# One 512-column product for both parts of a split activation, in a kernel of two transformer blocks

## The chip, the core and the metric

The kernel runs on one core of a Trainium2 chip. Five engines work side by side: TensorE multiplies (the profile lists its matmuls as PE and its weight loads as PEld), VectorE (DVE) and ScalarE (ACT) compute on SBUF and PSUM, GpSimd (POOL) computes on SBUF, and SyncE (SP) issues DMAs. The metric is the device time of one execution in microseconds, the median over runs; lower is better.

## What is computed

The input is one sequence of 256 tokens with 1024 features, in float32. The reference is two blocks in a row:

```
x = x + mixers(rms_norm(x)) @ w_out                      # block 1: block attention, gated linear attention
x = x + (silu(h_gate) * h_val) @ w_ffn_down              # h = causal_dwconv(rms_norm(x) @ w_ffn_up)
x = rms_norm(x)
x = x + (sum over 4 branches: gate * branch) @ w_out_2   # block 2: conv, spatial gating, two attentions
x = x + (silu(g) * u) @ w_ffn_out_2                      # g, u = split(rms_norm(x) @ w_ffn_in_2)
```

Both feed-forward layers have 2816 hidden features. Seen as tiles of 128 x 128, all the weights together are 1888 tiles, 118 pieces of 1 MB with 16 tiles each. An up projection has 44 x 8 = 352 tiles, a down projection 8 x 22 = 176, and an output projection 8 x 8 = 64.

## The kernel before

Activations stand with the features in the partitions and the 256 tokens (`T`) in the free dimension, 1024 features as `KD` = 8 chunks and 2816 as `KF` = 22. The products have to be more exact than one pass in the matmul type float32r, so each operand is kept as two float32r parts that add up to the float32: a rounded part (hi, h) and the rest (lo, l). A product of a weight tile with a chunk of activations is then three matmuls of 256 columns into the same PSUM columns, by `mm3`:

```
PE.matmul(ps, lh, rh, ...)   # weight hi, activation hi    L185
PE.matmul(ps, lh, rl, ...)   # weight hi, activation lo    L186
PE.matmul(ps, ll, rh, ...)   # weight lo, activation hi    L187
```

`fm` runs `mm3` over the chunks of one output tile. `fm_pair` runs two output tiles of a bank at once and leaves the last chunk of both to the end, because after a norm's sum that chunk is ready last. `tm` has tokens in the partitions of the result.

The weights are one stream, in the order in which they are used. SyncE's queue loads pieces of 1 MB into three buffers. `split_to` cuts a piece in two halves of 8 tiles; ScalarE casts a half to its hi part (L154), VectorE subtracts to get the lo part (L155). There are five buffers of hi and of lo, and a half is split `AHEAD` = 4 halves before its first tile is used. Engines take their instructions in an order that is fixed when the program is built: a scheduler runs through the program with estimated times and writes the order out for each engine.

PSUM has eight banks. Four are the rotating buffers `mm` of the main products, one bank each (`mm_tile`), four belong to the attention work (`at_tile`).

`Boundary` handles a norm between layers. `add(d, ps)` adds output tile d to the residual stream X (VectorE, L387), then `scaled` writes X times the norm's weights as hi (ScalarE, L282) and lo (VectorE, L283), without the norm's 1/rms; a sum of squares runs beside it. The next layer starts on these raw parts. In `gated_ffn` the first `HELD` = 6 hidden pairs j use the raw parts, and their results are multiplied by 1/rms (`rb`) afterwards, by VectorE straight from PSUM (tile `held`, L745). Meanwhile `normed` makes normed parts chunk by chunk: GpSimd multiplies by rb (L290), ScalarE and VectorE write hi and lo (L291, L292), and the hidden pairs from the seventh on use these. Each hidden pair j is 16 tiles into one bank, gate in the lower 256 columns and value in the upper. In block 2 `swiglu_emit` applies Silu to the lower half of the bank (L1102), multiplies by the upper (L1103), and `split_from` writes hi and lo of the hidden tile (L217, L218). The down projection runs 22 tiles for each of 8 output tiles; in block 2 its result is added to X (L1107) and sent out by DMA (L1108).

Hence the order of the second half of the program: branch products of block 2, second output projection, norm, second up projection, second down projection. Work of the attention parts runs between the tiles of the main stream in both mixers.

Of the kernel before, what the change touches and what calls it, by code (L numbers as in the profile page):

```python
# [26 lines left out]
HELD = 6  # L27
# [25 lines left out]
def block_kernel(ctx: ExitStack, tc: tile.TileContext, xT, wst, sm_d, cs_d, lv_d, gup_d, out, dbg=None):  # L53
# [73 lines left out]
    class Stream:  # L127
# [17 lines left out]
        def split_to(self, n):  # L145
            while self.split < min(n, 2 * N_PIECES):
                i, h = divmod(self.split, 2)
                self.load_to(i + 3)
                hi = parts.tile([128, 1024], F32R, name="hi", tag="hi")
                lo = parts.tile([128, 1024], F32R, name="lo", tag="lo")  # L150
# [8 lines left out]
                self.hl[self.split] = (hi, lo)  # L159
                self.split += 1  # L160

        def tiles(self, n=1):
            """The next n tiles of 128 x 128, side by side."""
# [5 lines left out]
            hi, lo = self.hl[h]  # L169
            return hi[:, t * 128:(t + n) * 128], lo[:, t * 128:(t + n) * 128]  # L170
# [13 lines left out]
    def mm3(ps, lh, ll, rh, rl, start, stop, **kw):  # L184
        PE.matmul(ps, lh, rh, start=start, stop=False, **kw)  # L185
        PE.matmul(ps, lh, rl, start=False, stop=False, **kw)  # L186
        PE.matmul(ps, ll, rh, start=False, stop=stop, **kw)  # L187

    def fm(ps, xh, xl, ks, start=True, stop=True, steps=0, **kw):
        ks = list(ks)  # L190
        for n, k in enumerate(ks):
            wh, wl = st.tiles()
            mm3(ps, wh, wl, xh[:, k, :], xl[:, k, :], start and n == 0, stop and n == len(ks) - 1, **kw)
            if n % 4 == 3:
                pump(steps)

    def fm_pair(ps, xh, xl, between=None):
        """Two tiles at once, the last chunk of both at the end."""
        for n, (a, k) in enumerate([(a, k) for a in range(2) for k in range(KD - 1)] + [(0, KD - 1), (1, KD - 1)]):
            wh, wl = st.tiles()  # L200
            mm3(ps[:, a * T:(a + 1) * T], wh, wl, xh[:, k, :], xl[:, k, :], n == 0, k == KD - 1,
                skip_group_check=True)
# [3 lines left out]
    def tm(dests, xh, xl, steps=0):  # L206
        """Columns of the next 16 tiles, with the tokens in the partitions."""
        ws = [st.tiles(2) for _ in range(KD)]
        for i, ps in enumerate(dests):
            t = slice(i * 128, (i + 1) * 128)  # L210
            for k, (wh, wl) in enumerate(ws):
                mm3(ps, xh[:, k, t], xl[:, k, t], wh, wl, k == 0, k == KD - 1)
                if k % 4 == 3:
                    pump(steps)

# [5 lines left out]
    def bcast(cols, n, width, wk, tag, bufs):  # L221
        """cols [128 tokens, n]: the rows [n * width, 128 tokens] that hold them."""
# [4 lines left out]
    def inv_sqrt(v, n, wk, root=False):  # L227
        """1 / sqrt(v) from the tables (a logarithm and an exponential, or a root), then a step of Newton's."""
# [20 lines left out]
    def token_sums(rows):  # L249
        """The sums of rows [128, T] over the partitions, with the tokens in the partitions: [128, 2]."""  # L250
# [29 lines left out]
    def scaled(k, g, xh, xl):  # L280
        """Chunk k of the residual stream times the norm's weights, without the norm's 1/rms."""
        a = S.activation(xh[:, k, :], X[:, k, :], AF.Identity, scale=g[:, k:k + 1])  # L282
        b = V.scalar_tensor_tensor(xl[:, k, :], X[:, k, :], g[:, k:k + 1], f32(xh[:, k, :]), op0=ALU.mult,  # L283
# [3 lines left out]
    def normed(rb, g, xh, xl, wk):  # L287
# [983 lines left out]
```

## Time and profile before

| | |
|---|---|
| runs | 761.25, 760.78, 760.6 us, median 760.78 us |
| profiled execution, first to last instruction | 758.6 us; this span is the only time shown of that execution |
| median less span | 2.2 us |
| TensorE matmul, weight load busy | 740.3 us, 723.2 us |
| VectorE, ScalarE, GpSimd busy | 544.2, 416.5, 113.6 us |
| granted TensorE clock, mean | 0.998 |

Busy shares of TensorE say little here: a matmul's record is longer than the distance to the next one, so records overlap. What one matmul costs is read from starts: the distance from one start to the next, or a stage's length divided by its tiles. A stage's length is read from the first start of its moving operand (mh for the second output projection, yh and xh for the second up projection, hh for the down projections).

### The profile page before, as it was taken

To read this page: it belongs to the slowest core of one execution; us is meant where nothing else is said; L and a number is where in the kernel's file an instruction comes from. 1 tells how busy PE (TensorE), PEld (TensorE's weight loads), DVE (VectorE), ACT (ScalarE), POOL (GpSimd) and SP (SyncE) were. 2 spreads that over 40 slices of the span, in tenths; PEclk is the share of its full clock that TensorE was granted. 3 is DMA by queue.
4 is the path that set the end of the run, shared out by engine and by line. 5 is a ranking of instruction groups with operands and counts; after the bars stand their busy time and mean duration, and the time that the engine had idled before them with its cause. 6 is when DMAs were issued, how large, how long until landed. Compare 5 with 4: busy or idle time off the path is not lost.

```text
span 758.6 us, 14593 instructions
## 1 busy us (share of the span) xinstructions
PE 740.3 (98%) x6042; PEld 723.2 (95%) x6042; DVE 544.2 (72%) x821; ACT 416.5 (55%) x673; POOL 113.6 (15%) x125
## 2 busy tenths in 40 slices
PE   8987899999999999999999999999999999999998
PEld 7987788999999999999998999999999999999998
DVE  6689955799998775556775777766988955555441
ACT  7453576568676665545547467445467644444330
POOL 3067200114312111212000001010223100000000
PEclk9999999999999999999999999999999999999999
DMA  8733231454545545544443444455445555545630
GB/s 303 291 112 111 74 133 72 167 183 152 219 171 199 190 168 193 197 168 167 162 172 111 139 145 163 170 182 204 167 164 209 184 183 198 175 172 201 204 125 22
DMA packets 19812, 127.51 MB, mean 168 GB/s; under 512 B 2321, under 2 KB 3746, under 8 KB 5026
## 3 DMA queue, kind: packets, MB, share of 16 engines
q1 hardware_dynamic: 19602, 126.56, 46.8%
q8 instruction: 47, 0.77, 0.4%
q14 instruction: 19, 0.16, 0.1%
q10 hardware_dynamic: 144, 0.02, 0.0%
HBM read 125.52 MB, written 1.05 MB: 167 GB/s over the span
## 4 chain that ended last, share of the span: by engine, by line
PE 90%; DVE 6%; issue 1%; DMA 1%; ACT 1%; SPq 0%
PE mm L186 28%; PE mm L185 28%; PE mm L187 28%; DVE lo L155 2%; DVE rob L648 1%; PE at L371 1%; DMA X<-in_x 1%; PE at L662 1%; DVE AT L505 1%; PE at L363 1%; DVE Qb L526 0%; DVE xl L283 0%; DVE AT L537 0%; PE at L892 0%; ACT hi L154 0%
## 5 line engine op out<-in xcount | busy, mean ns | idle before, releaser
L155 DVE TENSOR_TENSOR lo<-raw,hi 128x1024 fp32r<-128x1024 f32 (+1 forms) x236 | 296.3, 1259 | 138.2 <-ACT hi L154 137.4
L154 ACT CAST hi<-raw 128x1024 fp32r<-128x1024 f32 (+1 forms) x236 | 244.0, 1039 | 225.6 <-PE mm L186 179.4
L185 PE MATMUL mm<-yh,hi 128*128 128x256 f32 x800 | 226.4, 284 | 0.1
L186 PE MATMUL mm<-yl,hi 128*128 128x256 f32 x800 | 226.1, 283 | 0.0
L187 PE MATMUL mm<-yh,lo 128*128 128x256 f32 x800 | 226.0, 283 | 0.0
L185 PE MATMUL mm<-xh,hi 128*128 128x256 f32 x544 | 154.4, 285 | 1.4 <-ACT hi L154 1.4
L186 PE MATMUL mm<-xl,hi 128*128 128x256 f32 x544 | 155.0, 286 | 0.1
L187 PE MATMUL mm<-xh,lo 128*128 128x256 f32 x544 | 154.1, 285 | 1.0 <-DVE lo L155 1.0
L186 PEld LDWEIGHTS mm<-yl,hi 128*128 128x128 f32 x800 | 153.1, 192 | 0.7 <-issue 0.6
L185 PEld LDWEIGHTS mm<-yh,hi 128*128 128x128 f32 x800 | 152.8, 192 | 0.9 <-issue 0.7
L187 PEld LDWEIGHTS mm<-yh,lo 128*128 128x128 f32 x800 | 153.1, 192 | 0.1
L185 PEld LDWEIGHTS mm<-xh,hi 128*128 128x128 f32 x544 | 104.4, 192 | 2.2 <-ACT hi L154 1.8
L187 PEld LDWEIGHTS mm<-xh,lo 128*128 128x128 f32 x544 | 104.0, 192 | 2.2 <-DVE lo L155 1.6
L186 PEld LDWEIGHTS mm<-xl,hi 128*128 128x128 f32 x544 | 104.3, 192 | 1.3 <-DVE xl L283 0.5
L186 PE MATMUL mm<-hl,hi 128*128 128x256 f32 x352 | 98.4, 280 | 0.0
L187 PE MATMUL mm<-hh,lo 128*128 128x256 f32 x352 | 98.4, 280 | 0.0
L185 PE MATMUL mm<-hh,hi 128*128 128x256 f32 x352 | 98.1, 280 | 0.0
L186 PEld LDWEIGHTS mm<-hl,hi 128*128 128x128 f32 x352 | 66.2, 188 | 0.0
L187 PEld LDWEIGHTS mm<-hh,lo 128*128 128x128 f32 x352 | 66.2, 188 | 0.0
L185 PEld LDWEIGHTS mm<-hh,hi 128*128 128x128 f32 x352 | 66.0, 188 | 0.0
L277 POOL TENSOR_TENSOR ssa<-ssa,sq 128x256 f32<-128x256 f32 x20 | 18.8, 942 | 119.9 <-ACT sq L276 119.3
L771 POOL TENSOR_TENSOR cv<-cv 128x256 f32<-128x256 f32 x22 | 22.5, 1025 | 82.8 <-DVE cv L768 73.2
(333 smaller groups left out, 960.5 us busy)
## 6 DMA issues: line engine op xcount, KB each, us to landing
raw<-in_w SPq DMA_DIRECT2D x115, 1024.0 KB, 4.8
raw<-in_w SPq DMA_DIRECT2D x3, 512.0 KB, 8.2
out<-X SPq DMA_DIRECT2D x8, 128.0 KB, 1.9
sm<-in_sm SPq DMA_DIRECT2D x1, 814.5 KB, 11.9
X<-in_x SPq DMA_DIRECT2D x3, 256.0 KB, 7.1
cs<-in_cs SPq DMA_DIRECT2D x1, 706.0 KB, 11.2
raw<-in_w SPq DMA_DIRECT2D x2, 256.0 KB, 4.0
X<-in_x SPq DMA_DIRECT2D x2, 128.0 KB, 3.3
```

What stands on the lines that cost most here:

```text
L154: a = S.copy(hi[:, c:c + step], raw[:, c:c + step])
L155: b = V.tensor_tensor(lo[:, c:c + step], raw[:, c:c + step], f32(hi[:, c:c + step]), op=ALU.subtract)
L185: PE.matmul(ps, lh, rh, start=start, stop=False, **kw)
L186: PE.matmul(ps, lh, rl, start=False, stop=False, **kw)
L187: PE.matmul(ps, ll, rh, start=False, stop=stop, **kw)
L277: (V if self.n >= 6 else G).tensor_tensor(self.s, self.s, q, op=ALU.add)
L363: PE.transpose(pts[hd][:, j * 128:(j + 1) * 128], Ps[hd][:, j * 128:(j + 1) * 128], ident)
L371: PE.matmul(o, vs_[hd][0], PTs[hd][:, 0:256], start=True, stop=False, skip_group_check=True)
L505: V.tensor_scalar(AT[:, n // 4, n % 4, :], ident, dg[:, n:n + 1], None, op0=ALU.mult)
L648: V.tensor_tensor(b[o:o + 64, :], p[i:i + 64, :], sinr[i:i + 64, :], op=ALU.mult)
L662: PE.matmul(ps[:, c:c + n], qb[:, a, hd, i * 128:(i + 1) * 128], kT[:, a, :n], start=True, stop=False, skip_group_check=True)
L771: G.tensor_tensor(c[0], c[0], c[1], op=ALU.mult)
```

## The change

In four places, the down projections of both blocks, the second up projection and the second output projection, the two products that share the weight's hi part become one. For that the two parts of an activation now stand side by side, `[128, k, 2, T]` (class `Pair`, names `xx`, `yy`, `hh`, `mm_`), and the first matmul takes both as 512 columns; its result fills a whole bank, hi times hi in the lower 256 columns and hi times lo in the upper. The third product, lo weights with the hi activations, adds to the upper half. The two halves of a bank are summed afterwards: at a residual sum by two additions of VectorE instead of one, and in the second up projection by a ScalarE copy of the upper halves of two banks and one VectorE addition of the lower ones. There the 1/rms of the first six hidden pairs moves to GpSimd. All other places keep three matmuls of 256 columns.

PSUM's four `mm` buffers become two buffers of two banks (`mm_pair`). `mm_tile` gives out the two banks of such a buffer one after the other, so a buffer comes free when both banks have been read. The hi and lo parts of a weight half become one tile `hl` with five buffers, and in block 2's mixers two tiles (`u8a`, `u8b`) become one (`u16`). Elsewhere the diff renames (`xh, xl` to `x`, `mm3` to `mm_parts`) and drops comments.

```
-    mmp = ctx.enter_context(tc.tile_pool(name="mmp", bufs=4, space=PSUM))
+    mmp = ctx.enter_context(tc.tile_pool(name="mmp", bufs=2, space=PSUM))
+    spare = []
+    def mm_pair():
+        del spare[:]
+        return mmp.tile([128, 2, 512], F32, name="mm", tag="mm")
     def mm_tile():
-        return mmp.tile([128, 512], F32, name="mm", tag="mm")
+        if not spare:
+            p = mm_pair()
+            spare.append(p[:, 1, :])
+            return p[:, 0, :]
+        return spare.pop()
...
+    def both(ps, x, k, last):
+        w, b = st.tiles(), x.both(k)
+        PE.matmul(ps, w[:, 0, :], b.rearrange("p a t -> p (a t)"), start=(k == 0), stop=False, skip_group_check=True)
+        PE.matmul(ps[:, T:], w[:, 1, :], b[:, 0, :], start=False, stop=last, skip_group_check=True)
+    def fb(ps, x, n):
+        for k in range(n):
+            both(ps, x, k, k == n - 1)
+    def fb_pair(pss, x, between=None):
+        for n, (a, k) in enumerate([(a, k) for a in range(2) for k in range(KD - 1)] + [(0, KD - 1), (1, KD - 1)]):
+            both(pss[:, a, :], x, k, k == KD - 1)
+            if between and n == KD:
+                between()
+    def add_halves(dst, ps):
+        for a in range(2):
+            V.tensor_tensor(dst, dst, ps[:, a * T:(a + 1) * T], op=ALU.add)
...
         def add(self, d, ps):
-            V.tensor_tensor(X[:, d, :], X[:, d, :], ps, op=ALU.add)
-            behind = scaled(d, self.g, self.h, self.l)
+            if ps.shape[1] > T:
+                add_halves(X[:, d, :], ps)
+            else:
+                V.tensor_tensor(X[:, d, :], X[:, d, :], ps, op=ALU.add)
+            behind = scaled(d, self.g, self.raw)
...
-    def gated_ffn(nb, emit, finish):
+    def gated_ffn(nb, emit, finish, banks=False):
...
+                if banks:
+                    ps = mm_pair()
+                    if j == 0:
+                        fb_pair(ps, x, nb.sums)
+                    else:
+                        for a in range(2):
+                            fb(ps[:, a, :], x, KD)
...
+                if banks:
+                    t = wk.tile([128, 2, T], F32, name="held", tag="held", bufs=3)
+                    S.copy(t, ps[:, :, T:])
+                    V.tensor_tensor(t, t, ps[:, :, :T], op=ALU.add)
+                    if j < HELD:
+                        G.tensor_tensor(t, t, nb.rb[:, None, :].to_broadcast([128, 2, T]), op=ALU.mult)
+                    ps = t.rearrange("p a t -> p (a t)")
...
             for d in range(KD):
                 ps = mm_tile()
-                fm(ps[:, :T], hh, hl, range(KF))
-                finish(d, ps[:, :T], wk)
+                fb(ps, h, KF)
+                finish(d, ps, wk)
...
-        ps = mm_tile()
-        fm_pair(ps, mh, ml)
+        ps = mm_pair()
+        fb_pair(ps, m)
         for d in range(KD):
-            if d > 1:
-                ps = mm_tile()
-                fm(ps[:, :T], mh, ml, range(KD))
-            nb_.add(d, ps[:, T:] if d == 1 else ps[:, :T])
+            nb_.add(d, ps[:, d, :] if d < 2 else last)
+            if 0 < d < KD - 1:
+                last = mm_tile()
+                fb(last, m, KD)
...
     def second_end(d, ps, wk):
-        V.tensor_tensor(X[:, d, :], X[:, d, :], ps, op=ALU.add)
+        add_halves(X[:, d, :], ps)
         nc.sync.dma_start(out=out[:, d, :], in_=X[:, d, :])
...
-    gated_ffn(nb_, swiglu_emit, second_end)
+    gated_ffn(nb_, swiglu_emit, second_end, True)
```

## Rows read from the trace of the kernel before

**Rows 1.** Page, part 1: busy time of each engine, share of the span, instructions.
```profile
PE 740.3 (98%) x6042; PEld 723.2 (95%) x6042; DVE 544.2 (72%) x821; ACT 416.5 (55%) x673; POOL 113.6 (15%) x125
```

**Rows 2.** What TensorE waited for: total us, times, longest us.
```profile
PE at L533 <- DVE Qb L526: 10.0, 3, 4.6
PE mm L185 <- ACT hi L154: 1.4, 2, 1.2
```

**Rows 3.** Stretches: us, busy PE, PEld, DVE, ACT, POOL, clock, DMA share, GB/s.
```profile
544.20:566.00 21.80, 21.80 (x195) 21.80 (x194) 18.10 (x31) 12.20 (x22) 4.74 (x5) 1.00 0.42 147
566.00:693.10 127.10, 127.10 (x1060) 127.05 (x1059) 83.82 (x113) 67.28 (x102) 9.52 (x9) 1.00 0.53 191
```

**Rows 4.** Matmuls of one line by moving tile: ns min/median/max, first and last start.
```profile
L185 PE MATMUL mm<-mh,hi x64: 276/276/286, 544.2 to 565.6; 128*128 128x256 f32 x64
L185 PE MATMUL mm<-yh,hi x96: 280/283/468, 566.0 to 600.6; 128*128 128x256 f32 x96
L185 PE MATMUL mm<-hh,hi x176: 277/280/282, 693.1 to 754.7; 128*128 128x256 f32 x176
```

**Rows 5.** Timeline of TensorE: start us, us; the four 512-column products of line 932.
```profile
423.51 0.39 PE L932 MATMUL at<-h,nlater 128*128 128x512 f32 x1
423.74 0.28 PE L185 MATMUL mm<-yh,hi 128*128 128x256 f32 x1
423.86 0.28 PE L186 MATMUL mm<-yl,hi 128*128 128x256 f32 x1
...
428.53 0.39 PE L932 MATMUL at<-l,nlater 128*128 128x512 f32 x1
428.87 0.28 PE L185 MATMUL mm<-yh,hi 128*128 128x256 f32 x1
...
452.89 0.39 PE L932 MATMUL at<-h,nlater 128*128 128x512 f32 x1
453.23 0.28 PE L187 MATMUL mm<-yh,lo 128*128 128x256 f32 x1
...
460.18 0.39 PE L932 MATMUL at<-l,nlater 128*128 128x512 f32 x1
460.51 0.28 PE L187 MATMUL mm<-yh,lo 128*128 128x256 f32 x1
```

**Rows 6.** Timeline of TensorE: products with four-column weights (21 more between).
```profile
353.56 0.28 PE L186 MATMUL at<-yl,wfh 128*4 128x256 f32 x1
...
356.12 0.28 PE L187 MATMUL at<-yh,wfl 128*4 128x256 f32 x1
```

**Rows 7.** Groups by form: busy us, mean ns, then idle before and its releaser.
```profile
L1049 DVE TENSOR_TENSOR gate<-mm,rb 128x512 f32<-128x512 f32 x16 | 11.0, 689 | 6.1 <-PE mm L187 6.1
L387 DVE TENSOR_TENSOR X<-X,mm 128x256 f32<-128x256 f32 x24 | 9.5, 414 | 13.6 <-PE mm L187 13.6
L154 ACT CAST hi<-raw 128x1024 fp32r<-128x1024 f32 x232 | 241.7, 1046 | 224.8 <-PE mm L186 179.4 <-issue 31.6 <-PE mm L187 8.9
L519 ACT ACTIVATE E<-Dl 128x512 f32<-128x512 f32 x6 | 3.8, 632 | 11.3 <-DVE Dl L517 6.8 <-DVE Qb L526 4.5
L521 POOL TENSOR_TENSOR Kl<-gqk,E 128x512 f32<-128x512 f32 x6 | 9.1, 1516 | 0.2 <-ACT E L519 0.2
```

**Rows 8.** Timeline of VectorE, the end of the program.
```profile
755.26 0.42 DVE L1107 TENSOR_TENSOR X<-X,mm 128x256 f32<-128x256 f32 x1 [7.32 <-PE mm L187]
```

**Rows 9.** Timeline of VectorE around the second output projection's end.
```profile
553.22 1.23 DVE L155 TENSOR_TENSOR lo<-raw,hi 128x1024 fp32r<-128x1024 f32 x1 [2.66 <-ACT hi L154]
554.97 1.08 DVE L387 TENSOR_TENSOR X<-X,mm 128x256 f32<-128x256 f32 x3 [0.52 <-PE mm L187]
...
569.28 0.48 DVE L283 SCALAR_TENSOR_TENSOR yl<-X,sm,yh 128x256 fp32r<-128x256 f32 x1 [0.58 <-ACT yh L282]
```

**Rows 10.** Timeline of GpSimd behind that projection.
```profile
580.34 5.00 POOL L290 TENSOR_TENSOR xt<-X,rb 128x256 f32<-128x256 f32 x4 [14.17 <-DVE rb L242]
...
590.78 0.86 POOL L290 TENSOR_TENSOR xt<-X,rb 128x256 f32<-128x256 f32 x1 [0.76 <-DVE xl L292]
```

More of the change, by code (lines that the diff above doesn't have):

```diff
@@ L182, in block_kernel, with __init__, both @@
     V.tensor_copy(causalb, cst("causal"))
[L184 to L189, printed above, removed]
+    class Pair:
+        def __init__(self, t):
+            self.t, self.h, self.l = t, t[:, :, 0, :], t[:, :, 1, :]
+        def both(self, k):
+            return self.t[:, k]
@@ new lines, in fb, with fm @@
+    def fb(ps, x, n):
[9 more added lines that the diff above has]
+            V.tensor_tensor(dst, dst, ps[:, a * T:(a + 1) * T], op=ALU.add)
+    def fm(ps, x, ks, start=True, stop=True, steps=0, **kw):
@@ L190, in fm, with fm_pair @@
         ks = list(ks)
         for n, k in enumerate(ks):
-            wh, wl = st.tiles()
-            mm3(ps, wh, wl, xh[:, k, :], xl[:, k, :], start and n == 0, stop and n == len(ks) - 1, **kw)
+            mm_parts(ps, st.tiles(), x.both(k), start and n == 0, stop and n == len(ks) - 1, **kw)
             if n % 4 == 3:
                 pump(steps)
-    def fm_pair(ps, xh, xl, between=None):
+    def fm_pair(ps, x, between=None):
         for n, (a, k) in enumerate([(a, k) for a in range(2) for k in range(KD - 1)] + [(0, KD - 1), (1, KD - 1)]):
-            wh, wl = st.tiles()
-            mm3(ps[:, a * T:(a + 1) * T], wh, wl, xh[:, k, :], xl[:, k, :], n == 0, k == KD - 1,
-                skip_group_check=True)
+            mm_parts(ps[:, a * T:(a + 1) * T], st.tiles(), x.both(k), n == 0, k == KD - 1, skip_group_check=True)
@@ L381, in __init__ @@
             self.g, self.then = g, then or new_x
-            self.h, self.l = (first or new_y)()
+            self.raw = (first or new_y)()
             self.ss = SumSq(nwk, "a")
@@ L443, in block_kernel @@
             for d in range(4):
-                wh, wl = st.tiles()
-                mm3(pss[d // 2][:, d % 2 * T:(d % 2 + 1) * T], wh, wl, xh[:, k, :], xl[:, k, :],
-                    k == 0 and d % 2 == 0, k == KD - 1, skip_group_check=True)
+                mm_parts(pss[d // 2][:, d % 2 * T:(d % 2 + 1) * T], st.tiles(), x.both(k),
+                         k == 0 and d % 2 == 0, k == KD - 1, skip_group_check=True)
         r = rstd_cols(token_sums(ss.s), 2, 1.0 / D, nwk)
@@ L687, in block_kernel @@
                 ps = mm_tile()
-                fm(ps[:, :T], xh, xl, range(KD), steps=2)
+                fm(ps[:, :T], x, range(KD), steps=2)
                 rotary(ps, a, is_q)
@@ L695, in block_kernel @@
             ps = mm_tile()
-            fm(ps[:, :T], xh, xl, range(KD), steps=2)
+            fm(ps[:, :T], x, range(KD), steps=2)
             V.tensor_tensor(sg[:, e, :], ps[:, :T], rb, op=ALU.mult)
@@ L711, in block_kernel @@
                 a = accs[d // 2]
-                fm(a[:, (d % 2) * T:(d % 2 + 1) * T], yh, yl, range(4 * half, 4 * half + 4),
+                fm(a[:, (d % 2) * T:(d % 2 + 1) * T], y, range(4 * half, 4 * half + 4),
                    start=(half == 0 and d % 2 == 0), stop=(half == 1), steps=2, skip_group_check=True)
@@ L847, in proj @@
             for j in range(2):
-                fm(ps[:, j * T:(j + 1) * T], xh, xl, range(KD), steps=steps)
+                fm(ps[:, j * T:(j + 1) * T], x, range(KD), steps=steps)
             return ps.rearrange("p (c t) -> p c t", c=2)
-        q4 = wk.tile([128, 2, 2, 2, T], F32, name="q4", tag="u8a")
+        qkv = wk.tile([128, 14, T], F32, name="qkv", tag="u16")
+        q4 = qkv[:, 0:8, :].rearrange("p (n a h) t -> p n a h t", n=2, a=2)
         G.memset(q4, 0.0)
         qf, qs = q4[:, 0], q4[:, 1]
-        kv4 = wk.tile([128, 3, 2, T], F32, name="kv4", tag="u8b")
-        ks, vfx, vs = (kv4[:, n] for n in range(3))
+        ks, vfx, vs = (qkv[:, 8 + 2 * n:10 + 2 * n, :] for n in range(3))
         kf = wk.tile([128, 2, 2, T], F32, name="kf")
```

125 lines of the change are left out of this document (61 added, 64 removed).

## The prediction

> **What bounds the kernel now.** I start with the busy times [rows 1]: TensorE's matmuls and weight loads both cover nearly the whole span. Records overlap, so this shows only that TensorE is always at work, not at what speed. Next, what TensorE waited for [rows 2]: 10 us on VectorE inside the linear attention of the first block, 1.4 us on weight casts, and no entry at all for a PSUM buffer that was not free. Then the stretches of the changed stages [rows 3]: in the second output projection and the second up projection TensorE and its loads are busy from edge to edge at a granted clock of 1.00, VectorE 18.1 of 21.8 us and 83.8 of 127.1 us. So these stages last as long as their matmuls follow each other, and the price of a tile is a stage's length over its tiles. From first starts [rows 4]: the up projection runs from 566.0 (yh) to 693.1 (hh), 127.1 us / 352 = 0.361 us a tile; the down projection's first products start from 693.1 to 754.7, 175 steps, 0.352 us; the output projection takes 566.0 - 544.2 = 21.8 us / 64 = 0.341 us. A third of 0.361 is 0.120 us for one 256-column product.
>
> **What the change does to a tile.** It removes one matmul and one weight load of three and keeps the columns: 512 + 256 instead of 3 x 256. It pays only if something in those 0.120 us belongs to the matmul and not to its columns. The trace has four 512-column float32r products, each between products of 256 [rows 5]. The first starts at 423.51 and the next at 423.74: 0.23 us, less than 2 x 0.12. So 256 more columns cost 0.11, and about 0.01 is paid once per matmul. The change's pattern is exactly such a pair, one product of 512 and the 256 behind it. From the start of the 512 to the start of what follows the 256 the four pairs take 0.35, 0.34, 0.34 and 0.33 us. I take 0.343: single distances are read to 0.01, and a steady pattern of pairs may not do better than isolated ones. Bounds: 0.350 and 0.330, the longest and the shortest.
>
> The Trainium skill ("TensorE: Matmul & The Clock Gate", Back-to-back issue gap) speaks against the change: a matmul costs N / 2.4 + 2.5 ns, so one matmul less saves 2.5 ns a tile, an estimated 1.9 us over 768 tiles. The trace disagrees with its size, 0.120 us where it gives 0.109 for 256 columns.
>
> Is the extra the weight load, then? Products with four-column weights [rows 6] go from 353.56 to 356.12 in 22 steps, 0.116 us each: almost the same with hardly any load. So the load is not what a 256-column product waits for, and hiding more of it brings little.
>
> Sum for TensorE, each tile at 0.343: up projection 352 x 0.018 = 6.3 us; both down projections 352 x 0.009 = 3.2 us (the first has the same 176 tiles, and I take the second's pace for both); output projection 64 x -0.002 = -0.1 us. Together 9.4 us. At 0.350: 3.9 + 0.7 - 0.6 = 4.0 us; at 0.330: 10.9 + 7.7 + 0.7 = 19.3 us.
>
> **What it adds.** Every residual sum gets a second addition. One of 128 x 256 from PSUM takes 414 ns [rows 7].
>
> At the end of the program nothing covers it: the last addition starts right behind the last matmul [rows 8], then comes the last DMA. +0.4 us.
>
> In the first down projection a chunk has 22 tiles, 7.5 us, and the norm behind it still has fourteen tiles before it needs the last chunk: hidden.
>
> In the second output projection two things can wait. First, PSUM: there are now two buffers of two banks, and d = 4 needs the buffer of d = 0 and 1 back. It starts after 32 tiles, at 544.2 + 32 x 0.341 = 555.1. VectorE's first residual additions start at 554.97, because VectorE stands before a weight subtraction (553.22) for 2.66 us [rows 9]. With four additions of 0.41 us, TensorE would wait up to 1.5 us if this order stays, nothing if the scheduler puts them first. I take 0.7. Second, the last chunk for the next layer: its lo part is written by 569.76 [rows 9] and needed after fourteen tiles, at 566.0 + 14 x 0.361 = 571.1, 1.3 us of slack; at the faster pace 1.0 us. Eight more additions are 3.3 us on an engine with 3.7 us free. Bounds: no wait when only its own 0.4 us is added, 2.3 us when all 3.3 arrive there. I take 0.7. Behind those additions stand weight subtractions, but four halves of weights (32 tiles, 11 us) are ready ahead.
>
> In the second up projection a hidden pair takes 16 x 0.343 = 5.5 us. VectorE has 83.8 / 22 = 3.8 us of work in it and gets one addition of 512 columns, 0.69 us (L1049 in [rows 7]); that is 4.5, and less where it gives up the 1/rms product. ScalarE has 67.3 / 22 = 3.1 us and gets a copy of 512 columns, by the nearest row 0.63 us (L519 in [rows 7]): 3.7. Both are hidden under the matmuls with 1 us to spare; without that cover each 0.1 us beyond 5.5 would cost 2.2 us over 22 pairs. The copy and the addition free the PSUM buffer within some 3 us, and TensorE needs it 5.5 us later.
>
> The 1/rms products on GpSimd (1.5 us each for 512 columns, L521 in [rows 7]) share it with the eight products of the norm, which run from 580.34 to 591.6 [rows 10]. Taken in between they cost nothing; a bad order is a rival below. I take 0.3 us.
>
> In the mixers a mm buffer now returns when both its banks are read. No wait of TensorE for such a buffer shows before [rows 2]; VectorE waits for TensorE to fill them (6.1 us at L1049 in [rows 7]). Bounds 0 and about 1 us; I take nothing. The cast of a new weight half waits for the lo product too now, 0.12 us later; ScalarE already waits 179 us for TensorE there (L154 in [rows 7]), under cover of the four halves. Loads come a twentieth faster, on DMA engines that are half idle [rows 3]. A scheduler that writes a new order in the first block can move a microsecond either way; it has no term.
>
> Costs: 0.4 + 0.7 + 0.7 + 0.3 = 2.1 us. Net 9.4 - 2.1 = 7.3 us.
>
> The span of the profiled execution is 758.6 us and the median of the runs 760.8; the 2.2 us lie outside the first and last instruction and stay. Forecast: 760.8 - 7.3 = 753.5 us.
>
> **The rivals.** *Columns alone set the pace.* Then a 512-column product is 2 x 0.12 = 0.24 us, a tile stays at 0.36 or 0.35, and only the costs are left: 760.8 + 2.1 = 762.9 us, slower. It decides from 0.24 on. For it: the fixed part is one hundredth of a microsecond, read from four places, and none of the four has its moving operand in the x or y tiles that the up projection reads. Against it: none of the four pairs reaches 0.36. By the 2.5 ns a matmul of the Trainium skill (the section named above) it would be an estimated 761.0 us; no row here shows a distance that small over the columns' time.
>
> *The fixed part vanishes.* If with two loads under 768 columns only columns count, a tile takes 3 x 0.11 = 0.33 us: -19.3 + 2.1, 743.6 us. For it: one pair of four reads 0.33, and a lo load has all of a 512-column product to hide under. Against it: four-column loads still gave 0.116, and in the first pair 0.12 followed the 0.23.
>
> *GpSimd comes late in the second up projection.* If it does all eight norm products first, the first 1/rms product ends at 591.6 + 1.5 = 593.1, Silu and product (0.4 us each, as L387 in [rows 7]) at 593.9. Tile `held` has three buffers, so the copy of the fourth pair starts there and its PSUM buffer is free at 593.9 + 0.63 + 0.69 = 595.2; the sixth pair would start at 566.0 + 5 x 5.5 = 593.5. TensorE waits 1.7 us, and as much again if casts queue behind the waiting Silu on ScalarE and the weights run out. In place of the 0.3 us that is 3.4 us: 756.6 us. For it: four norm products already run back to back as soon as rb is there [rows 10]. Against it: they also wait for their readers, and gaps open between them.
>
> **How the numbers follow.** Forecast 0.70, with a range of its own from 748 (a tile of 0.335) to 759 (0.350 and these costs); columns alone 0.08; the fixed part vanishes 0.12; GpSimd late 0.10. Leaving out 0.08 above and most of the 0.12 below, the range is 745 to 759.5 us. A measurement of this kernel can tell about 0.2%, 1.5 us: faster is below 759.3, slower above 762.3. The forecast (0.68 of 0.70), the vanishing part (0.12) and most of GpSimd's case (0.08) are faster, together 0.88. Same: 0.03 of the columns, 0.02 of GpSimd, 0.01 of the forecast, 0.06. Slower: 0.05 of the columns, 0.01 of the forecast, 0.06.
>
> **What would show it.** Right: in the second up and the down projections a 512-column product is followed after 0.22 to 0.23 us and a 256 after 0.11 to 0.12; the up stage lasts near 121 us and each down projection near 60.4; the last matmul is followed by two additions. Wrong: 0.24 behind a 512; a wait of TensorE for a reader of mm or for a lo part near the second output projection of more than 3 us; GpSimd as releaser in front of Silu; or a first block whose length moves by more than 2 us. The prediction fails if the four pairs are no measure for operands in other tiles.

## The result and the profile after

The changed kernel takes 819.4 us (median of 4 runs, 817.98 to 820.5) where the kernel before takes 760.7 us on the same chip: ratio 1.0772, 95% interval [1.0757, 1.0788]. It is slower by 58.7 us. The forecast was 753.5 us, and no rival went past 763.

The page of the changed kernel first: busy times of TensorE and VectorE, and the granted clock of TensorE in 40 slices of the span.

```profile
PE 754.8 (92%) x5274; PEld 696.9 (85%) x5274; DVE 567.4 (69%) x861; ACT 429.4 (52%) x695; POOL 117.5 (14%) x131
...
PEclk9999999979999889999999999999999999999999
```

TensorE has 768 matmuls fewer than in [rows 1], as the change says, and its busy share fell from 98% to 92%. The clock row falls below 9 in three slices (164 to 184 and 266 to 307 us); its mean is 0.976 against 0.998. What TensorE waited for (engine, tile and line, releaser: us in total, times, longest us):

```profile
PE mm L205 <- DVE cv L820: 13.2, 3, 4.5
PE mm L205 <- DVE held L798: 9.7, 2, 6.1
PE mm L205 <- ACT hl L165: 8.5, 5, 2.2
...
PE mm L213 <- DVE X L229: 3.2, 3, 1.5
PE mm L213 <- DVE held L792: 2.7, 2, 2.2
```

L205 is the first of the three 256-column products of `mm_parts`; L213 and L214 are the 512 and the 256 of the new `both`. L820 (convolution), L798 and L792 (`held`, in the first and in the second block) and L229 (residual sum) are VectorE's reads of an `mm` buffer; L165 casts weights. So TensorE now waits for PSUM, in stretches that the change does not even convert: L205 is the unchanged form. In [rows 2] there is no such entry.

Now the stages by windows (us, then busy time of PE, PEld, DVE, ACT and POOL, clock, DMA share, GB/s). The kernel before: first up, first down, mixers of block 2, second down; its other two stages are in [rows 3].

```profile
150.10:278.50 128.40, 128.20 (x1060) 127.32 (x1059) 117.08 (x179) 88.54 (x147) 31.76 (x32) 1.00 0.52 185
278.50:340.30 61.80, 61.80 (x529) 61.80 (x528) 36.87 (x44) 31.84 (x47) 10.68 (x12) 1.00 0.53 188
340.30:544.20 203.90, 203.90 (x1649) 196.49 (x1649) 149.09 (x229) 111.14 (x163) 19.77 (x24) 1.00 0.46 161
693.10:754.90 61.80, 61.80 (x529) 61.80 (x528) 25.32 (x27) 19.48 (x20) 0.00 (x0) 1.00 0.39 135
```

The changed kernel: first up, first down, mixers of block 2, second output projection, second up, second down.

```profile
150.40:316.60 166.20, 134.02 (x1013) 131.99 (x1011) 110.95 (x170) 86.84 (x141) 25.94 (x31) 0.91 0.38 134
316.60:391.30 74.70, 71.35 (x416) 62.73 (x417) 42.35 (x56) 33.94 (x51) 11.12 (x13) 0.98 0.47 168
391.30:598.80 207.50, 203.82 (x1633) 194.51 (x1632) 149.49 (x234) 111.06 (x163) 17.80 (x24) 1.00 0.45 158
598.80:624.20 25.40, 23.16 (x130) 19.54 (x129) 21.54 (x36) 13.38 (x23) 4.21 (x5) 1.00 0.48 166
624.20:752.30 128.10, 125.19 (x709) 108.31 (x708) 99.58 (x126) 77.50 (x121) 19.19 (x15) 1.00 0.51 181
752.30:814.40 62.10, 61.13 (x353) 53.54 (x351) 28.57 (x35) 19.90 (x21) 0.00 (x0) 1.00 0.39 134
```

The first up projection went from 128.4 to 166.2 us and the first down projection, whose first tiles run among the last of the up, from 61.8 to 74.7: +50.7 of the span's +60 us. Mixers and output projection add 3.6 us each, the second up 1.0, the second down 0.3, the end 0.5 and the part ahead of the first up projection 0.3. Two windows there have a clock under 1.00. Its levels are 2.4 and 1.2 GHz, so 0.91 over 166.2 us is some 30 us at the lower one, and 0.98 over 74.7 us some 3.

What such a wait looks like, on TensorE's timeline (start us, us, instruction, in brackets the idle time and its releaser):

```profile
264.06 0.28 PE L207 MATMUL mm<-yy,hl 128*128 128x256 f32 x1
268.87 0.55 PE L205 MATMUL mm<-yy,hl 128*128 128x256 f32 x1 [4.53 <-DVE cv L820]
269.22 0.41 PE L206 MATMUL mm<-yy,hl 128*128 128x256 f32 x1
269.43 0.41 PE L207 MATMUL mm<-yy,hl 128*128 128x256 f32 x1
```

4.5 us of nothing, then products 0.21 us apart where they were 0.12: the clock had fallen to 1.2 GHz. ScalarE around it (L818 reads a half of a hidden pair's bank for the convolution, L165 casts weights):

```profile
252.87 0.56 ACT L818 ACTIVATE cv<-mm,sm 128x256 f32<-128x256 f32 x1 [0.41 <-DVE cv L820]
...
263.66 0.56 ACT L818 ACTIVATE cv<-mm,sm 128x256 f32<-128x256 f32 x1 [1.83 <-PE mm L207]
264.12 1.98 ACT L165 CAST hl<-raw 128x1024 fp32r<-128x1024 f32 x2
266.00 0.56 ACT L818 ACTIVATE cv<-mm,sm 128x256 f32<-128x256 f32 x1
```

And VectorE (L819 and L820 read the bank, L166 subtracts weights):

```profile
264.25 0.48 DVE L819 SCALAR_TENSOR_TENSOR cv<-mm,sm,cv 128x255 f32<-128x255 f32 x1 [1.17 <-ACT cv L818]
264.77 0.48 DVE L820 SCALAR_TENSOR_TENSOR cv<-mm,sm,cv 128x254 f32<-128x254 f32 x1
265.19 2.36 DVE L166 TENSOR_TENSOR hl<-raw,hl 128x1024 fp32r<-128x1024 f32 x2
267.46 0.87 DVE L819 SCALAR_TENSOR_TENSOR cv<-mm,sm,cv 128x255 f32<-128x255 f32 x2
268.25 0.86 DVE L820 SCALAR_TENSOR_TENSOR cv<-mm,sm,cv 128x254 f32<-128x254 f32 x2
```

Between 253.4 and 263.7 ScalarE reads no bank (the rows left out are casts and SBUF work). A pair takes 5.8 us in the kernel before (128.4 us / 22). Here the reads of two pairs come in one burst, the next burst starts 10 us after its end, and inside it two casts (264.12) and two subtractions (265.19) stand ahead of the read that TensorE needs. Distances of more than 1 us between starts come twelve times in the first up and down projections and sum to 38.7 us. The first is the longest, 6.34 us; the next four are 4.81, 4.81, 4.39 and 3.90 us. The first two end with L798. From 211 us on they come about every second hidden pair: four end with L820 (2.7 to 4.8 us), the other six with a weight cast, L165 (1.1 to 2.5 us).

### The profile page after: what moved, and what is told of

Read it like the earlier page. It is cut to its first block, busy times and chain, and to the rows that moved or that the text cites. A ratio compares the mean times of both kernels' runs of the same rounds, so it can differ in the third digit from the quotient of the medians.

```text
span 818.6 us, 13059 instructions
## 1 busy us (share of the span) xinstructions
PE 754.8 (92%) x5274; PEld 696.9 (85%) x5274; DVE 567.4 (69%) x861; ACT 429.4 (52%) x695; POOL 117.5 (14%) x131
## 4 chain that ended last, share of the span: by engine, by line
PE 76%; DVE 14%; ACT 4%; issue 3%; DMA 1%; POOL 1%; SPq 0%; ACTq 0%; POOLq 0%; DVEq 0%
PE mm L213 20%; PE mm L205 14%; PE mm L207 13%; PE mm L206 13%; PE mm L214 10%; DVE hl L166 4%; ACT hl L165 2%; ACT cv L818 1%; DVE cv L819 1%; DVE rob L690 1%; DVE xx L334 1%; DVE cv L820 1%; DMA X<-in_x 1%; PE at L413 1%; DVE X L229 1%
## 5 line engine op out<-in xcount | busy, mean ns | idle before, releaser
L166 DVE TENSOR_TENSOR hl<-raw,hl 128x1024 fp32r<-128x1024 f32 (+1 forms) x236 | 292.2, 1244 | 131.6 <-ACT hl L165 131.0
L165 ACT CAST hl<-raw 128x1024 fp32r<-128x1024 f32 (+1 forms) x236 | 243.5, 1040 | 187.7 <-PE mm L207 106.5
L205 PE MATMUL mm<-yy,hl 128*128 128x256 f32 x704 | 202.4, 289 | 21.9 <-DVE cv L820 13.2
L206 PE MATMUL mm<-yy,hl 128*128 128x256 f32 x704 | 202.3, 288 | 0.0
L207 PE MATMUL mm<-yy,hl 128*128 128x256 f32 x704 | 201.2, 287 | 0.0
L205 PEld LDWEIGHTS mm<-yy,hl 128*128 128x128 f32 x704 | 137.4, 196 | 24.5 <-issue 15.5
L206 PEld LDWEIGHTS mm<-yy,hl 128*128 128x128 f32 x704 | 137.8, 196 | 0.5 <-issue 0.2
L207 PEld LDWEIGHTS mm<-yy,hl 128*128 128x128 f32 x704 | 137.5, 196 | 0.5 <-issue 0.4
L213 PE MATMUL mm<-hh,hl 128*128 128x512 f32 x352 | 124.3, 397 | 6.0 <-ACT hl L165 2.5
L205 PE MATMUL mm<-xx,hl 128*128 128x256 f32 x288 | 86.1, 299 | 15.8 <-DVE held L798 9.7
L214 PE MATMUL mm<-hh,hl 128*128 128x256 f32 x352 | 98.9, 282 | 0.0
L213 PE MATMUL mm<-xx,hl 128*128 128x512 f32 x256 | 90.8, 399 | 0.7 <-DVE held L792 0.5
L207 PE MATMUL mm<-xx,hl 128*128 128x256 f32 x288 | 84.3, 294 | 1.4 <-DVE hl L166 1.4
L213 PEld LDWEIGHTS mm<-hh,hl 128*128 128x128 f32 x352 | 66.7, 190 | 21.9 <-ACT hl L165 3.0
L206 PE MATMUL mm<-xx,hl 128*128 128x256 f32 x288 | 84.0, 292 | 0.0
L205 PEld LDWEIGHTS mm<-xx,hl 128*128 128x128 f32 x288 | 57.5, 200 | 18.2 <-DVE held L798 6.3
L214 PE MATMUL mm<-xx,hl 128*128 128x256 f32 x256 | 71.9, 281 | 0.0
L214 PEld LDWEIGHTS mm<-hh,hl 128*128 128x128 f32 x352 | 66.9, 190 | 0.4 <-DVE hl L166 0.3
L213 PEld LDWEIGHTS mm<-xx,hl 128*128 128x128 f32 x256 | 48.1, 188 | 13.3 <-DVE held L792 0.8
L207 PEld LDWEIGHTS mm<-xx,hl 128*128 128x128 f32 x288 | 57.1, 199 | 2.5 <-DVE hl L166 2.0
L206 PEld LDWEIGHTS mm<-xx,hl 128*128 128x128 f32 x288 | 57.6, 200 | 0.6 <-DVE xx L325 0.2
L214 PEld LDWEIGHTS mm<-xx,hl 128*128 128x128 f32 x256 | 48.4, 189 | 0.0
```

Of the source, the lines that this page charges most:

```text
L165: a = S.copy(hi[:, c:c + step], raw[:, c:c + step])
L166: b = V.tensor_tensor(lo[:, c:c + step], raw[:, c:c + step], f32(hi[:, c:c + step]), op=ALU.subtract)
L205: PE.matmul(ps, w[:, 0, :], x[:, 0, :], start=start, stop=False, **kw)
L206: PE.matmul(ps, w[:, 0, :], x[:, 1, :], start=False, stop=False, **kw)
L207: PE.matmul(ps, w[:, 1, :], x[:, 0, :], start=False, stop=stop, **kw)
L213: PE.matmul(ps, w[:, 0, :], b.rearrange("p a t -> p (a t)"), start=(k == 0), stop=False, skip_group_check=True)
```

## The experiments

Medians; the ratio is to the kernel before, timed beside it. Stage lengths and steps are from each run's trace.

| kernel | median us | ratio [95% interval] |
|---|---|---|
| changed kernel | 819.4 | 1.0772 [1.0757, 1.0788] |
| e1 single banks | 765.49 | 1.0067 [1.0052, 1.0082] |
| e2 pairs only | 842.39 | 1.1088 [1.106, 1.1116] |
| e3 changed, three products | 818.4 | 1.0763 [1.0745, 1.0781] |
| e5 two buffers | 786.03 | 1.034 [1.0321, 1.0359] |
| e9 first banks | 789.79 | 1.0391 [1.0367, 1.0415] |
| e4 single banks, three products | 763.9 | 1.005 [1.0036, 1.0064] |
| e7 down projections only | 759.96 | 0.9999 [0.9991, 1.0008] |
| e8 output projection only | 768.22 | 1.0097 [1.0077, 1.0116] |
| e6 second up in part, both downs | 758.45 | 0.9978 [0.997, 0.9987] |
| e10 e6 with hi and lo apart | 757.45 | 0.9959 [0.9945, 0.9972] |
| e11 joined hi and lo only | 761.26 | 1.0011 [1.0002, 1.002] |

The first theory was that the two-bank buffers cost the 60 us; the rivals were the 512-column products themselves and, within the buffers, their mere number.

**e1, the change with four buffers of one bank.** The second up projection takes two of them and empties each by itself.

```
-    mmp = ... tile_pool(name="mmp", bufs=2, space=PSUM)
-    (mm_pair, spare: two banks of one buffer)
+    mmp = ... tile_pool(name="mmp", bufs=4, space=PSUM)
+    def mm_pair():
+        return [mm_tile(), mm_tile()]
...
-                    S.copy(t, ps[:, :, T:])
-                    V.tensor_tensor(t, t, ps[:, :, :T], op=ALU.add)
+                    for a in range(2):
+                        S.copy(t[:, a, :], ps[a][:, T:])
+                        V.tensor_tensor(t[:, a, :], t[:, a, :], ps[a][:, :T], op=ALU.add)
```

> The changed kernel with its four PSUM buffers of one bank back: the second up projection takes two of them and empties each bank by itself (two copies and two additions of 256 columns instead of one of 512). The 512-column products, the tile layout and all else stay. Theory P (the two-bank buffer is the cost: the first product into its second bank waits until its first bank has been read): the waits on readers of mm are gone and the tiles' own pace in the changed trace is left, 96 x 13 ns + 256 x 7 ns in the up projection, 352 x 4 ns in the down projections, -64 x 13 ns in the output projection, some 3.6 us less than before: 755 to 759 us. Theory Q (the 512-column products starve or slow the program): about 819 us. Theory R (too few PSUM buffers, whatever their shape): 755 to 759 us too.

Measured 765.49 us. 54 of the 59 us are gone with the buffers; the first up projection is back (window as above):

```profile
151.70:280.20 128.50, 128.21 (x1060) 127.37 (x1059) 117.19 (x179) 88.36 (x148) 36.80 (x33) 1.00 0.53 186
```

But it is above its expectation and still slower than before: a second loss was hidden behind the first. Its place, on TensorE's timeline in the second output projection:

```profile
556.17 0.28 PE L206 MATMUL mm<-mm__4794,hl 128*128 128x256 f32 x1
559.26 0.52 PE L205 MATMUL mm<-mm__4794,hl 128*128 128x512 f32 x1 [2.81 <-DVE X L221]
559.58 0.41 PE L206 MATMUL mm<-mm__4794,hl 128*128 128x256 f32 x1
559.79 0.63 PE L205 MATMUL mm<-mm__4794,hl 128*128 128x512 f32 x1
```

and VectorE at the same time (L158 subtracts weights, L221 adds to the residual stream):

```profile
555.10 1.23 DVE L158 TENSOR_TENSOR hl<-raw,hl 128x1024 fp32r<-128x1024 f32 x1 [3.65 <-ACT hl L157]
556.24 1.41 DVE L221 TENSOR_TENSOR X<-X,mm 128x256 f32<-128x256 f32 x4
557.57 1.22 DVE L158 TENSOR_TENSOR hl<-raw,hl 128x1024 fp32r<-128x1024 f32 x1
558.70 1.07 DVE L221 TENSOR_TENSOR X<-X,mm 128x256 f32<-128x256 f32 x3
```

The fifth chunk needs the bank of the first one back. VectorE waits for a cast, subtracts a weight half (555.10), then adds the lower halves of four chunks (x4, 556.24), subtracts another weight half (557.57), and only then adds the first chunk's upper half (558.70): this order is the built program's. Two additions a chunk instead of one let the scheduler deal them out so that no bank is free until the fifth. TensorE waits 2.8 us, and the products after it start at a distance of 0.32 and 0.21 us, at 1.2 GHz. The output projection takes 27.2 us against 21.8. A second wait, 2.3 us behind `held`, stands before the sixth pair of the second up projection, with 3.4 us at 1.2 GHz behind it.

**e2, the kernel before with the paired buffers and no 512-column product.**

```
-    mmp = ... tile_pool(name="mmp", bufs=4, space=PSUM)
+    mmp = ... tile_pool(name="mmp", bufs=2, space=PSUM)
+    (mm_pair and mm_tile with spare, as in the change)
```

> The kernel before with one part of the change alone: its PSUM buffers become two of two banks and are handed out bank by bank. All products stay at 256 columns. Theory P: most of the loss is there without any 512-column product, 805 to 830 us. Theory Q: no change, 760 to 763 us. Theory R: as P.

Measured 842.39 us, worse than the whole change. The waits of TensorE:

```profile
PE mm L196 <- DVE cv L779: 31.1, 9, 5.0
PE mm L196 <- DVE held L756: 13.3, 4, 5.9
```

The first up projection takes 176.3 us. The buffers alone do the damage, and where all products have 256 columns it comes again in the second up and down projections (140.0 and 68.5 us against 127.1 and 61.8).

**e3, the changed kernel with the 512-column product cut into two of 256.**

```
-        PE.matmul(ps, w[:, 0, :], b.rearrange("p a t -> p (a t)"), ...)
+        PE.matmul(ps[:, :T], w[:, 0, :], b[:, 0, :], ...)
+        PE.matmul(ps[:, T:], w[:, 0, :], b[:, 1, :], ...)
```

> The changed kernel with its 512-column product taken apart into two of 256 that write the same two halves of the bank; buffers, order of the program and sums stay. Theory P: as slow as the changed kernel or a few us slower, 819 to 826 us, since a tile gets 4 to 13 ns dearer in most places. Theory Q: back near the kernel before, 762 to 770 us. Theory R: as P.

Measured 818.4 us. Within the intervals the wide product changes nothing in this kernel's time: the loss does not come from it.

**e5, the kernel before with two buffers of one bank** (two more banks, aside, for the first output projection, which needs four accumulators at once).

```
-    mmp = ... tile_pool(name="mmp", bufs=4, space=PSUM)
+    mmp = ... tile_pool(name="mmp", bufs=2, space=PSUM)
+    accp = ... tile_pool(name="accp", bufs=2, space=PSUM)
```

> The kernel before with only two PSUM buffers of one bank for the main products instead of four (two more banks stand aside for the output projection of the first block alone, which needs four at once). All products stay. Theory P (it is the shared buffer, not the number): TensorE still has a buffer to go on with, 761 to 775 us. Theory R (the number of buffers): as slow as the changed kernel or slower, 810 to 830 us. Theory Q: 760 to 763 us.

Measured 786.03 us, between the two expectations. The waits of TensorE:

```profile
PE mm L186 <- DVE cv L769: 8.5, 15, 2.9
...
PE mm L186 <- DVE held L746: 6.4, 2, 3.4
```

With half the banks TensorE has shorter waits, 0.4 us each but for a few, and the whole costs 25 us. With all four banks, but paired, it costs 82 (e2). So the number of buffers is one part, and something in the pairing is a larger one.

**e9, two buffers of two banks of which the main products use only the first.**

```
     def mm_tile():
-        return mmp.tile([128, 512], F32, name="mm", tag="mm")
+        return mm_pair()[:, 0, :]
```

> The kernel before with two buffers of two banks of which only the first bank is ever given out (the second banks are used by the linear attention's accumulators alone). Theory N (what cost e2_pairs_only its 56 us over e5_two_buffers was that the first product into a second bank waits for the readers of the first bank of the same buffer): with no second bank in use that wait is gone and only the small number of buffers is left, 783 to 790 us as e5_two_buffers, and TensorE's waits in the first up projection are below 1 us each. Theory S (the two-bank shape itself costs, in addressing or in the order the scheduler writes for it): 830 to 845 us, with waits of 3 to 5 us every second hidden pair as in e2_pairs_only.

Measured 789.79 us. The waits of TensorE:

```profile
PE mm L192 <- DVE held L752: 9.7, 2, 6.7
PE mm L192 <- DVE cv L775: 8.7, 15, 3.0
```

Leaving the second banks empty makes the kernel 53 us faster than using them. This separates shape from sharing: a two-bank buffer by itself behaves nearly as a one-bank buffer (3.8 us above e5), and it is the use of the second bank that costs. The time is the one that theory N gave, but not all waits are below 1 us as it said: the longest of each row above, 6.7 and 3.0 us, stand in the first up projection, and e5 has both too (3.4 and 2.9 us). So a wait for `held` there belongs to two buffers as such.

In the built program of the changed kernel the first product into a second bank waits on the semaphores of the engines that read the first bank of the same buffer. The first wait, 6.34 us, is in front of such a product, which needs L798's read of the first bank. The later waits for L820 stand elsewhere. In the order that the scheduler wrote for TensorE, a second bank that still has to wait comes behind the first bank of the other buffer. So it is filled just before its own buffer is needed again, and the first product into that buffer then waits until L820 has read the second bank. By this reading dependencies are kept for the buffer, not the bank, and the four banks work as two that are also filled and emptied by turns. A program in which only that dependency is missing was not tried.

**e4, e1 with three products of 256** (the edit of e3 on e1).

> The kernel of run e1 (single banks) with its 512-column product taken apart into two of 256, nothing else. It asks what the product itself is worth where TensorE rarely waits. Theory T (a tile costs what the clean starts of e1 show, 0.347 against 0.360 us in the up projection, 0.348 against 0.352 in the down projections, 0.353 against 0.340 in the output projection): 352 x 13 + 352 x 4 - 64 x 13 ns = 5.1 us slower than e1, 769 to 772 us. Rival U (the columns alone set the pace, as the pairs' twin comparison of e3 with the changed kernel suggests, 818.4 against 819.4): as e1, 764.5 to 766.5 us.

Measured 763.9 us, below both expectations and not slower than e1 (the intervals overlap). The output projection takes 23.7 us instead of 27.2. VectorE begins the weight subtraction ahead of its additions at 553.84, where e1 has 555.10, and TensorE waits 1.6 us with no stretch at 1.2 GHz behind it, where e1 has 2.8 us and then 3.4 us at 1.2 GHz. Both expectations left that wait as in e1. Why the cast before the subtraction comes earlier is not settled. The wait before the sixth pair is gone as well.

Stage by stage the wide product does gain time. In e1 its tiles in the sixteen normed pairs of the second up projection follow each other after 0.347 us (ns min/median/max, first and last start):

```profile
L205 PE MATMUL mm<-xx,hl x256: 392/395/403, 610.1 to 698.6; 128*128 128x512 f32 x128
```

In e4 they do so after 0.360 us, and a down projection takes 60.9 us in e1, 61.8 in e4. The two waits of e1 and their stretches at 1.2 GHz eat this.

**e7, the wide product in the two down projections only; e8, in the second output projection only** (both with four single banks).

```
e7, e8:
-    gated_ffn(nb_, swiglu_emit, second_end, True)
+    gated_ffn(nb_, swiglu_emit, second_end)
e7, the output projection as before:
-        fb_pair(ps, m)
+        fm_pair(ps, m)
e8, the down projections as before:
-                fb(ps, h, KF)
-                finish(d, ps, wk)
+                fm(ps[:, :T], h, range(KF))
+                finish(d, ps[:, :T], wk)
```

> One part of the change alone, with single banks: 512-column products in the two down projections and nowhere else. Theory T: each down projection lasts 60.9 us instead of 61.9, and 0.4 us is added at the end: 758.9 us, 758.2 to 759.6. Rival U: 760.5 to 761.5 us.

> One part of the change alone, with single banks: the 512-column products of the second output projection and nowhere else. Theory T (its fifth chunk waits until VectorE has read the first, its clock halves behind that, and its tiles are 13 ns dearer): the stage lasts 27.1 us instead of 21.8 as in e1, 765 to 767 us. Rival (what e1 lost there came from the scheduler's order for the up projection behind it): 760 to 762 us.

Both came out a little above the first theory's expectation. e7 took 759.96 us: each down projection 60.9 us instead of 61.8, less 0.4 us at the end, but the median shows hardly any of that gain. Its profile has 152.4 instead of 150.1 us ahead of the first up projection; it is of the longest of the eleven runs, 761.49 us, so how much of this the median has is not shown. e8 took 768.22 us: the output projection 28.4 us, with the same 2.8 us behind `X` and 6.8 us at 1.2 GHz. That use of the change only loses.

**e6, what is left of it.** e1 with the output projection and the first six hidden pairs of the second up projection back at three products into one bank, 1/rms on VectorE as before.

```
+                two = banks and j >= HELD
-                if banks:
+                if two:
...
-                    if j < HELD:
-                        G.tensor_tensor(t, t, nb.rb[:, None, :].to_broadcast([128, 2, T]), op=ALU.mult)
```

> The kernel of e1 with the second output projection and the first six hidden pairs of the second up projection back at three products of 256 in one bank, and 1/rms back on VectorE; 512-column products stay in the other sixteen hidden pairs and in both down projections. It takes away the two places where e1 still waited for a reader of mm (3.1 and 2.6 us, each followed by a stretch at half clock). Theory T: 760.5 - 256 x 13 ns - 2.0 us of the two down projections + 0.4 us for the last addition = 755.6 us, 754.5 to 757. Rival U: 760.5 to 762 us, no gain left.

Measured 758.45 us, 0.2% faster than before. Its first down, second output, second up and second down projections (windows as above):

```profile
279.60:340.50 60.90, 60.90 (x353) 53.60 (x352) 39.95 (x51) 31.66 (x47) 12.03 (x12) 1.00 0.54 190
544.40:566.00 21.60, 21.60 (x193) 21.60 (x192) 17.85 (x30) 12.04 (x21) 5.59 (x5) 1.00 0.45 149
566.00:691.60 125.60, 125.60 (x806) 113.49 (x805) 98.79 (x145) 78.12 (x134) 8.90 (x8) 1.00 0.55 193
691.60:752.50 60.90, 60.90 (x354) 53.58 (x352) 28.67 (x35) 19.68 (x20) 0.00 (x0) 1.00 0.40 136
```

It is above its expectation, but below both kernels. None of these stages has a clock under 1.00 or a gap of more than 0.6 us. The downs are each 0.9 us shorter, the sixteen converted pairs together 1.7, the end 0.5 longer.

**e10 and e11, the weight parts in two tiles again, and joined alone.**

```
e10, on e6 (e11 is the reverse on the kernel before):
-                hl = parts.tile([128, 2, 1024], F32R, name="hl", tag="hl")
-                hi, lo = hl[:, 0, :], hl[:, 1, :]
+                hi = parts.tile([128, 1024], F32R, name="hi", tag="hi")
+                lo = parts.tile([128, 1024], F32R, name="lo", tag="lo")
```

> The kernel of e6_best with the hi and lo parts of a weight half in two tiles again, five buffers of each, as in the kernel before. In e6_best the part of the program ahead of the first up projection lasted 151.1 us, in e7_down_only 152.4, in the kernel before 150.1, and the changed kernel keeps both parts of a half in one tile, so that the next cast waits for the lo product too. Theory H (the joined tile costs that about 1 us): 757.2 to 757.9 us, the part ahead of the first up projection near 150.1 us. Theory O (that part moves with whatever order the scheduler happens to write, 148.9 to 152.4 us over all kernels so far): 756.5 to 760.5 us, and the second half of the program unchanged from e6_best (out 21.7, up 125.5, down 60.9 us).

> The kernel before with nothing changed but the hi and lo parts of a weight half in one tile of two. Theory H (the joined tile costs about 1 us in front of the first up projection): 761.2 to 762.2 us, that part near 151.1 us. Theory O (only the order moves): 759.5 to 762.5 us with that part anywhere from 149 to 152.5 us; the stages from the first up projection on as before (128.4, 61.8, 203.8, 21.7, 127.2, 61.8 us).

e10 took 757.45 us, the lowest median of all, and e11 761.26 us. Both medians agree with about 1 us for the joined tile; the interval of e11 alone runs from 0.2 to 1.5 us. But each lies in the ranges of both theories, so these runs do not tell them apart, and where the time is lost is not settled: the part ahead of the first up projection was 151.6 us in e11 and 150.8 in e10, and in both profiles over 10 us of it were at 1.2 GHz.

## Why the prediction was wrong

**The step that failed** is "In the mixers a mm buffer now returns when both its banks are read ... Bounds 0 and about 1 us; I take nothing." It was wrong by 50 to 60 us, in three ways.

*Place.* Of the stages that keep their products it looked at the mixers alone. `mm_tile` also feeds the first block's up projection, which the change does not convert, and 50.7 of the 60 us fell there and in the down projection interleaved with it. The prediction's own list of signs had this one: a first block whose length moves by more than 2 us. It moved by 51.

*Cause.* It read "No wait of TensorE for such a buffer shows before [rows 2]" as slack. That row shows only that four separate banks were enough; e5 shows that two are not (+25 us). And the step took the two banks of a buffer as independent until the buffer's return. e2 and e9 show that they are not: with second banks in use 842, without 790 us. A shared buffer costs at its second half, which waits for the reads of the first, and again when it comes back, since that half is filled and read last.

*Consequence.* It priced a wait as itself. Between the waits the reads of two pairs come in bursts, the weight casts come late too (8.5 us of waits for L165; [rows 2] has 1.4 us for casts), and behind the waits the clock falls. Some 33 us of the two windows ran at 1.2 GHz, 7 of them inside the waits (a clock of 0.74 over the 6.34 us of the first, for one). At 0.21 instead of 0.12 us a product the other 26 are worth 26 x 0.09 / 0.21 = 11 us; with 37 us of waits (38.7 less twelve normal steps) that is 48 us, and the two stages grew by 50.7. The split is worked out, not measured by itself.

**The tile price had the right mechanism and the wrong size.** Forecast 0.343 us (0.330 to 0.350) for a 512 and the 256 behind it. The second down projection of the changed kernel (ns min/median/max, first and last start):

```profile
L213 PE MATMUL mm<-hh,hl x176: 391/392/496, 752.2 to 814.1; 128*128 128x512 f32 x176
L214 PE MATMUL mm<-hh,hl x176: 278/280/284, 752.5 to 814.4; 128*128 128x256 f32 x176
```

From 752.2 to 814.1 with one wait of 1.0 us that is 0.348 a tile; in e6 60.6 us / 175 = 0.346. There the 512 takes 0.230 us and the 256 behind it 0.116. In the second up projection the changed kernel's first six pairs go at 0.347 a tile as well; in its other sixteen the 512 takes 0.236, 0.353 a tile, against 0.360 before. The sixteen pairs of e6 gained the same, 1.7 us / 256 = 0.007, but those of e1 0.013. In the output projection it is also 0.353, against 0.341: dearer. The four pairs of [rows 5] were each read to 0.01 us, and the gain per tile that they were to give was itself only 0.009 to 0.018. The steady streams make of the 9.4 us of the sum some 4 (two downs 0.9 each, 96 tiles x 0.013 = 1.2, 256 x 0.007 = 1.8, the output projection 64 x 0.012 = -0.8), or 5.5 with e1's 0.013 for the sixteen pairs. The condition was named, "if the four pairs are no measure for operands in other tiles", and taken too lightly. By the 2.5 ns a matmul of the Trainium skill ("TensorE: Matmul & The Clock Gate", Back-to-back issue gap), which that section gives for a matmul by itself and not for a stream with weight loads, it was an estimated 1.9 us; the traces show 5 to 13 ns a tile in the up and down projections, and a loss in the output projection.

**The end** was right: the two last additions take 0.88 us (x2) where [rows 8] has 0.42.

```profile
814.69 0.88 DVE L229 TENSOR_TENSOR X<-X,mm 128x256 f32<-128x256 f32 x2 [7.99 <-PE mm L214]
```

**The output projection's PSUM wait** was found at the right place, the fifth chunk behind VectorE's weight subtraction, and sized at 0.7 with 1.5 as its bound. The changed kernel waits 1.5 us there and 0.7 once more; with single banks it is 2.8 us and a stretch at 1.2 GHz (e1, e8). The bound counted four additions in a row; the order written in e1 was four lower halves, a weight subtraction, and then the upper ones.

**GpSimd late** was a rival with a chance of 0.10. The wait comes where it put it, before the sixth pair, 2.2 us long (L792 in the waits). But GpSimd is not late. Its timeline (L794 is the 1/rms product) and ScalarE's (L791 copies the upper halves, L259 casts a hidden tile):

```profile
643.76 5.16 POOL L794 TENSOR_TENSOR held<-held,rb 128x512 f32<-128x512 f32 x3
```

```profile
651.81 0.41 ACT L259 CAST hh<-cv 128x256 fp32r<-128x256 f32 x1 [2.95 <-DVE cv L1152]
652.12 0.58 ACT L791 COPY held<-mm 128x512 f32<-128x512 f32 x1
```

By 648.9 three 1/rms products are done; the copy at 652.12 stands behind the cast at 651.81, which waits for VectorE's product (L1152). It is ScalarE's queue that holds the copy back, behind VectorE. And VectorE is late beside GpSimd (L334 writes a lo part of the normed activations):

```profile
644.80 4.41 DVE L334 SCALAR_TENSOR_TENSOR xx<-xt,sm,xx 128x256 fp32r<-128x256 f32 x3
656.42 0.87 DVE L334 SCALAR_TENSOR_TENSOR xx<-xt,sm,xx 128x256 fp32r<-128x256 f32 x2
```

The three that ran during the 1/rms products took 1.5 us each, as long as one such product, the two later ones 0.47: 3.1 us more, and TensorE waited 2.2. So the rival had the right engine and the wrong way. That GpSimd's work is what stretched them is read from these times; no run changes it alone. e6 leaves those pairs on VectorE and has no wait.

**The other rivals.** That columns alone set the pace (762.9 us) is wrong for the up and down projections, though e1 lands near its time for other reasons. The fixed part does not vanish: no stream went below 0.346 us.

## What to carry to other kernels

Before a rotating buffer is made larger and rarer, list every stage that takes from it, changed or not, and ask when each part of it may be written again; a missing wait in the profile says that the present number is enough, not that there is slack. Consistent bubbles, one gap that repeats along the engine that should be saturated, can mean too few buffers, as the Trainium skill says ("Perfetto Trace Analysis", Optimization Strategy), and the waits every second pair here are that; four single banks cured them (e1), and taking the wide product apart did not (e3). A gain of a hundredth of a microsecond a tile is measured on a steady stream of that very pattern before a kernel is rebuilt for it.

## What the runs showed of the hardware

Short waits can cost more than their length: behind waits of 2.3 and 2.8 us in e1 TensorE ran 3.4 us each time at 1.2 GHz, while the waits of 0.4 us in e5's up projection, one of 1.6 us in e4 and also one of 2.9 us in e5 were followed by none. The length alone does not tell which.

The same 512-column product takes 0.230 us with `hh` or `yy` as its moving operand and 0.235 in the output projection; with `xx` it takes 0.236 in the changed kernel and in e6, but 0.232 in e1. A 256 behind it takes 0.116 to 0.118. Where all products have 256 columns, each takes 0.120 in the up, 0.117 in the down and 0.113 in the output projections. So the operand alone does not decide; why they differ stays open.

VectorE's lo part of 128 x 256 took 0.47 us by itself and 1.5 us each of three times beside a GpSimd product of 512 columns.
